# Columns of the second layer's h made before the LayerNorm, h in halves, and the small experts' outputs as split parts in a two-layer hybrid block

## The chip, the cores and the metric

The kernel runs on one core of a Trainium2 chip. The metric is the device time of one execution in microseconds (us), less is better. A core has five engines with their own instruction streams: TensorE (PE; its weight loads are shown as PEld), VectorE (DVE), ScalarE (ACT), GpSimd (POOL) and SyncE (SP), which here issues nearly all DMA transfers on one queue. They wait for one another by semaphores. TensorE's granted clock is given as a share of full speed.

## The reference

T = 256 tokens of width D = 1024, in float32, two layers. Each layer normalizes its tokens with an adaptive LayerNorm (scale and shift from `c @ w_ada + b_ada`), runs three mixers on the result (retention, a state-space mixer and sliding-window attention), projects their outputs back to D, adds the gated result to the input times ALPHA, and normalizes; then the same with a feed-forward part. Layer 0 has a dense SwiGLU of width 2816, layer 1 a mixture of 8 experts of width 3584, of which each token takes two:

```python
def _swiglu(h, wg, wu, wd):
    return (jax.nn.silu(h @ wg) * (h @ wu)) @ wd

def _moe(h, w_router, b_router, wg, wu, wd):
    ...
    top_v, top_i = lax.top_k(logits, TOP_K)
    top_w = jax.nn.softmax(top_v, -1)
    gates = jnp.sum(jax.nn.one_hot(top_i, N_EXPERTS, dtype=jnp.float32) * top_w[..., None], axis=1)
    out = jnp.zeros_like(t)
    for e in range(N_EXPERTS):
        out = out + gates[:, e:e + 1].astype(t.dtype) * _swiglu(t, wg[e], wu[e], wd[e])
    return out.reshape(Bn, L, D)
```

## The kernel before, in words

**Products.** An fp32 operand that is to be multiplied fast is split into two fp32r parts, the rounded value (a copy on ACT, L326) and what is left of it (a subtraction on DVE, L327). `mm3` (L395 to L397) then makes three matmuls: high by high, high by low, low by high. A matmul on fp32 operands as they are is one instruction that takes TensorE longer.

**Layer 0 and the boundaries.** Weights come in blocks of 1 MB over SP's queue into a ring of slots. `out_proj` and the end of `dense_ffn` call `follow(t, acc)` of `next_h` (L605) for each half t of the tokens. It forms the sum R, its statistics on DVE (L583 to L594), the reciprocal root on POOL (L575, L596) and the normalization on ACT (L603). For t = 1 it then makes the next h: `make_ht` calls `h_rows`, which transposes R in eight blocks on TensorE (L502), applies scale and shift from the columns `ac` (L508 on ACT, for k4 = 1 of t = 1 L510 on DVE), and after both halves `make_ht` writes the parts h1 (ACT, L491) and h2 (DVE, L492). `affine_cols` (L632) computes `ac` in a few tiny DVE instructions; at the second boundary (the end of the feed-forward part of layer 0) it is called from within `follow`. `affine_rows` (L626) then multiplies and shifts R itself on POOL (L623, L624), two instructions over 128x1024 for each t, with the rows in a tile of the tag "pair", which the gate rows (`ga`, L465) take next. These stretches run in the order in which they are written (a manual schedule), each engine by itself; the mixers are ordered by a scheduler. `behind()` adds an order of what is issued within it behind instructions named before; it works between instructions on one engine.

**The experts.** Tokens are gathered by rank of the experts. Four of them (ranks 1 to 4, called B) have up to 128 rows and weights that are split as above; the four others (ranks 0, 5, 6, 7, called S) have at most 64 rows and multiply by the raw fp32 weights, with two halves of the columns side by side on the partitions (`up_small` L1505, `down_small` L1537). Each expert has 7 steps of 6 blocks of 1 MB, 336 blocks in all. `plan` (L1318) writes the order of the steps: S S B B, then B and S in turn, at the end two steps of the last S alone. `feed` issues loads as slots come free. Side work is queued: `later(n, f)` runs f after n ticks, a tick follows each piece of a step, and a wide tick takes one job (a few matmuls into a bank C) from `jobs` and collects it at the next tick.

**An expert's output.** A B expert's y is scaled by the gates on POOL, split, and scattered to the tokens by one-hot matmuls (L1562). An S expert's y is scaled on DVE into `yts` (L1586) and scattered by four plain fp32 matmuls with 64 rows (L1591). Of the last B expert, `parts_of_last` (L1662) splits the sum so far and y, and `sums_of_last` (L1684) adds them in PSUM with 16 matmuls (L1692, L1696) right behind its last down step. The last S expert adds its four matmuls (L1776) to these banks, and `finish` normalizes and writes the output.

Of the kernel before, what the change touches and what calls it, by code (L numbers as in the profile page):

```python
# [42 lines left out]
SCALE_AT = 2  # L43

# [8 lines left out]
WIDE = {"": (2,), "S": (0, 1, 2, 3), "BS": (0, 1, 2, 3)}  # L53
# [113 lines left out]
def _layout(a):  # L167
# [16 lines left out]
    out["crow"] = a["c"]  # L184
    cm, ak, tm, zz = [], [], [], []
# [24 lines left out]
def block_stack_kernel(ctx: ExitStack, tc: tile.TileContext, I, out, coff, poff, cap=P):  # L210
# [42 lines left out]
    crep = W("crep").rearrange("p (k m) -> p k m", k=NK)  # L253
# [241 lines left out]
    def h_rows(hp, t, R, ac):  # L495

        hts = []
        for k4 in range(2):
# [12 lines left out]
            hts.append(ht)  # L511
        return hts
# [75 lines left out]
    def row_scale(st):  # L588
# [7 lines left out]
        nc.gpsimd.tensor_tensor(rs[:, 1:2], rs[:, 2:3], rs[:, 0:1], op=MULT)  # L596
# [551 lines left out]
    def route(hp, late, ahead, first, R, ac, g, xold):  # L1148
# [11 lines left out]
        def logits(t):  # L1160
            hts = h_rows(hp, t, R, ac)
# [156 lines left out]
    def plan(kind):  # L1318
# [6 lines left out]
        for c in ORDER[kind]:  # L1325
# [34 lines left out]
    def moe(mp, own, pair, hold, ahead, xs, sv, gate, cint, svr, gater, offi, room, big, ac, acc, gf):  # L1360
# [18 lines left out]
        def fetch(ex):  # L1379

            ex["rows"] = mp.tile([P, D], F32, tag="srows" if ex["small"] else "brows", name="rows", bufs=1)
            nc.gpsimd.indirect_dma_start(ex["rows"], None, xr, bass.IndirectOffsetOnAxis(ap=ex["ix"], axis=0))

        def turn_rows(ex, k4):

            ps = bankB()
            for c in range(4):
                k = 4 * k4 + c
                nc.tensor.transpose(ps[:, c * P:(c + 1) * P], ex["rows"][:, k * P:(k + 1) * P], ident)
# [27 lines left out]
        def slotted(ex, ps):  # L1417
# [5 lines left out]
            pt = mp.tile([P, 2, P], F32 if small else F32R, tag="pts" if small else "pt", name="pt", bufs=2)  # L1423
# [105 lines left out]
        def down_small(box, first, last, between=None, wide=False):  # L1529
            y = box["ex"]["y"]  # L1530
            for h in range(2):
# [8 lines left out]
                tick(wide)  # L1540

# [84 lines left out]
        def experts(kind):  # L1626
# [35 lines left out]
            def parts_of_last():  # L1662
# [13 lines left out]
                for j in range(2):  # L1676
                    s = slice(512 * j, 512 * j + 512)
                    yt = own.tile([P, 512], F32, tag=("yt", "yts")[j], name="yt")
# [20 lines left out]
            for op, r, b in ops[:-1]:  # L1699
# [34 lines left out]
                elif op == "Bturn":  # L1734
                    later(0, turned, box, turn(box))
                    while due:
                        tick()
# [11 lines left out]
                elif op == "Sup":  # L1749
                    boxes[r, b] = up_small(ex[r], WIDE.get(letter, ()))  # L1750
# [5 lines left out]
                elif op == "Sdown":  # L1756
# [6 lines left out]
                    if b == EX_STEPS - 1:  # L1763
                        later(0, output_small, ex[r])
# [7 lines left out]
            yt = own.tile([P, 512], F32, tag="yts", name="yt")  # L1772
            nc.vector.scalar_tensor_tensor(yt, small["y"], small["gs"], parts["gf2"], op0=MULT, op1=MULT)
            for t, j in itertools.product(range(2), range(2)):
                r = slice(64 * j, 64 * j + 64)
                nc.tensor.matmul(done[t, j], lhsT=small["pt"][r, t, :], rhs=yt[r, :], start=False, stop=True)  # L1776
# [69 lines left out]
    ada_pool = ada_scope.__enter__()  # L1846
    zb, quads = [], {}
# [73 lines left out]
    for l in range(2):  # L1921
# [27 lines left out]
        if l == 0:  # L1949
# [5 lines left out]
            def split_z():  # L1955
                ws.extend(split(I["wz"][1, 1, i], 4 * 324) for i in range(2))

            def ahead_z():
                box.append([bankA(), bankA()])
                tm_products(box[0], ws[0], 0, (0,), 324)  # L1960
# [13 lines left out]
            def zw():  # L1974
                for kh, t in ((1, 0), (0, 1), (1, 1)):
                    tm_products(box[0], ws[kh], kh, (t,), 324)
                return box[0]

            R = Rn2
            affine_rows(R, 0, 1)  # L1980
# [53 lines left out]
```

## Time and profile before

| | |
|---|---|
| median of 3 runs | 1399.26 us (1396.99 to 1399.78) |
| the profiled execution, its own time | 1399.08 us |
| its span, first to last instruction | 1397.2 us |
| mean granted clock of TensorE | 0.978 |
| PE / DVE / ACT / POOL busy | 96% / 66% / 47% / 6% |
| moved by DMA | 484.40 MB, mean 347 GB/s |

The profiled execution has 1.88 us outside its span. Layer 0 takes the first 396 us, the mixers and the routing of layer 1 the time up to about 510 us, the experts the rest. In all rows the first number is a start in us from the span's begin and the second a duration in us, if nothing else is said; "x8" joins eight instructions of one kind, and what stands in brackets is the idle time of the engine ahead of the row, and what ended it.

### The profile page before, as it was taken

To read this page: it belongs to the slowest core of one execution; us is meant where nothing else is said; L and a number is where in the kernel's file an instruction comes from. 1 tells how busy PE (TensorE), PEld (TensorE's weight loads), DVE (VectorE), ACT (ScalarE), POOL (GpSimd) and SP (SyncE) were. 2 spreads that over 40 slices of the span, in tenths; PEclk is the share of its full clock that TensorE was granted. 3 is DMA by queue.
4 is the path that set the end of the run, shared out by engine and by line. 5 is a ranking of instruction groups with operands and counts; after the bars stand their busy time and mean duration, and the time that the engine had idled before them with its cause. 6 is when DMAs were issued, how large, how long until landed. Compare 5 with 4: busy or idle time off the path is not lost. (4 is left out here: it accounts for less than half of the span.)

```text
span 1397.2 us, 20777 instructions
## 1 busy us (share of the span) xinstructions
PE 1335.7 (96%) x7956; PEld 1010.8 (72%) x7956; DVE 926.2 (66%) x1417; ACT 654.8 (47%) x948; POOL 88.7 (6%) x78
## 2 busy tenths in 40 slices
PE   7999899999899999999999999999999999999984
PEld 5867699999797885877676676677667777667641
DVE  3785789988778755956576665578556676665623
ACT  3743554453474533744454444456344555444510
POOL 0111020000121110003000000000000000000000
PEclk9999999999999978999999999999999999999998
DMA  9776668897543359999999999999999999999991
GB/s 388 291 297 244 250 241 330 353 382 284 202 168 127 109 223 392 383 368 410 417 420 421 420 421 420 421 421 420 421 421 420 420 421 421 421 420 421 421 397 43
DMA packets 69364, 484.40 MB, mean 347 GB/s; under 512 B 7744, under 2 KB 7744, under 8 KB 12800
## 3 DMA queue, kind: packets, MB, share of 16 engines
q1 hardware_dynamic: 67680, 477.41, 84.1%
q0 software_dynamic: 1568, 5.51, 1.1%
q8 instruction: 66, 1.08, 0.3%
q14 instruction: 50, 0.41, 0.1%
HBM read 480.52 MB, written 2.36 MB: 346 GB/s over the span
## 5 line engine op out<-in xcount | busy, mean ns | idle before, releaser
L327 DVE TENSOR_TENSOR w<-raw,w 128x1024 fp32r<-128x1024 f32 (+3 forms) x560 | 567.6, 1048 | 146.0 <-ACT w L326 137.9
L326 ACT ACTIVATE w<-raw 128x1024 fp32r<-128x1024 f32 (+3 forms) x560 | 484.7, 905 | 269.7 <-DMA raw<-in_wexp 110.9
L395 PE MATMUL B<-w,he 128*128 128x512 f32 x448 | 185.8, 415 | 3.2 <-ACT he L1404 3.2
L397 PE MATMUL B<-w,he 128*128 128x512 f32 x448 | 177.4, 396 | 0.0
L396 PE MATMUL B<-w,he 128*128 128x512 f32 x448 | 177.1, 395 | 0.0
L1505 PE MATMUL B<-raw,hs 128*64 128x256 f32 x1344 | 150.4, 382 | 0.0
L1505 PEld LDWEIGHTS B<-raw,hs 128*64 128x64 f32 x1344 | 95.1, 137 | 54.1 <-issue 6.3
L395 PE MATMUL A<-w,a 128*128 128x512 f32 x312 | 124.4, 399 | 0.0
L397 PE MATMUL A<-w,a 128*128 128x512 f32 x312 | 123.3, 395 | 0.0
L396 PE MATMUL A<-w,a 128*128 128x512 f32 x312 | 122.9, 394 | 0.0
L395 PEld LDWEIGHTS B<-w,he 128*128 128x128 f32 x448 | 84.7, 189 | 44.2 <-ACT w L326 18.7
L1518 DVE TENSOR_TENSOR sgs<-B,sgs 128x256 f32<-128x256 f32 x28 | 11.9, 425 | 150.8 <-ACT sgs L1515 150.8
L395 PE MATMUL B<-w,h 128*128 128x256 f32 (+1 forms) x368 | 107.1, 291 | 3.1 <-ACT h L491 3.1
L397 PE MATMUL B<-w,h 128*128 128x256 f32 (+1 forms) x368 | 106.0, 288 | 1.2 <-DVE h L492 1.1
L396 PE MATMUL B<-w,h 128*128 128x256 f32 (+1 forms) x368 | 105.5, 287 | 0.0
L1537 PE MATMUL A<-raw,as 128*64 128x512 f32 x448 | 101.5, 593 | 0.5 <-DVE as L1527 0.5
L1515 ACT ACTIVATE sgs<-B 128x256 f32<-128x256 f32 x28 | 10.7, 383 | 188.9 <-PE B L1505 188.9
L397 PEld LDWEIGHTS B<-w,he 128*128 128x128 f32 x448 | 84.6, 189 | 20.1 <-DVE he L1405 0.4
L396 PEld LDWEIGHTS B<-w,he 128*128 128x128 f32 x448 | 84.8, 189 | 15.8
L395 PE MATMUL A<-w,h 128*128 128x512 f32 (+1 forms) x176 | 68.6, 390 | 6.8 <-ACT h L491 4.4
L395 PEld LDWEIGHTS B<-w,h 128*128 128x128 f32 x368 | 71.5, 194 | 4.1 <-ACT h L491 3.3
L397 PEld LDWEIGHTS B<-w,h 128*128 128x128 f32 x368 | 71.4, 194 | 1.8 <-DVE h L492 1.8
(380 smaller groups left out, 1861.3 us busy)
## 6 DMA issues: line engine op xcount, KB each, us to landing
raw<-in_wexp SPq DMA_DIRECT2D x335, 1024.0 KB, 17.7
ada<-in_wada SPq DMA_DIRECT2D x45, 1024.0 KB, 6.6
raw<-in_wffn SPq DMA_DIRECT2D x33, 1024.0 KB, 7.2
raw<-in_wcm SPq DMA_DIRECT2D x8, 1024.0 KB, 6.9
raw<-in_wtm SPq DMA_DIRECT2D x8, 1024.0 KB, 6.8
raw<-in_wout SPq DMA_DIRECT2D x8, 1024.0 KB, 5.8
raw<-in_wz SPq DMA_DIRECT2D x8, 648.0 KB, 10.2
raw<-in_wada SPq DMA_DIRECT2D x3, 1024.0 KB, 11.6
```

Source lines behind the costliest of these rows:

```text
L326: nc.scalar.activation(w1[:, s], r, AF.Copy)
L327: eng.tensor_tensor(w2[:, s], r, w1[:, s].bitcast(F32), op=SUB)
L395: nc.tensor.matmul(ps, lhsT=a1, rhs=b1, start=start, stop=False, **kw)
L396: nc.tensor.matmul(ps, lhsT=a1, rhs=b2, start=False, stop=False, **kw)
L397: last["mm"] = nc.tensor.matmul(ps, lhsT=a2, rhs=b1, start=False, stop=stop, **kw)
L1505: nc.tensor.matmul(ps[64 * h:64 * h + 64, 256 * g:256 * g + 256], lhsT=ex["he"][k // 4][:, k % 4, :], rhs=raw[:, 512 * kk + 256 * h:512 * ...
L1515: nc.scalar.activation(box["sg"], ps[:, 0:256], AF.Silu)
L1518: nc.vector.tensor_tensor(box["sg"], ps[:, 256:512], box["sg"], op=MULT)
L1537: nc.tensor.matmul(y[64 * j:64 * j + 64, :], lhsT=box["a"][:, c, 64 * h:64 * h + 64], rhs=raw[:, 1024 * c + 512 * j:1024 * c + 512 * j + 512],
```

## The change

It has six parts. (1) The constant `crep` leaves the tile `par` and gets a tile and a load of its own. (2) `affine_cols(0, 1, 1, 0)` is called in `split_z`, ahead of the splits of the next weights, not within `follow`. (3) The two calls of `affine_rows` in layer 0 stand in `behind()`. (4) `h_rows` yields each half of h as soon as it is written, and `make_ht` splits it then. (5) For an expert with at most 64 rows, `fetch` takes 64 rows, not 128, and the transposes are 64 wide. (6) An S expert's y is scaled where it stands in PSUM, split into two fp32r parts that lie on the two halves of the partitions of one tile `st`, and scattered by one fp32r matmul of 128 rows for each of four outputs, with delays of `SMALL_AT` and `STEP_AT` ticks between the steps. At the end, the sums of the last B expert go behind the second-to-last `up` step of S, the `up` steps after the last B step take no jobs in their ticks (`WIDE["last"]`), and `down_small` collects a job right after the tick that issued it.

```diff
-    parts["crep"] = np.repeat(_cols(a["c"][0]), 32, axis=1)
...
+    out["crep"] = np.repeat(_cols(a["c"][0]), 32, axis=1)
...
-            hts.append(ht)
-        return hts
+            yield ht
...
-            nc.gpsimd.indirect_dma_start(ex["rows"], None, xr, bass.IndirectOffsetOnAxis(ap=ex["ix"], axis=0))
+            n = SMALL if ex["small"] else P
+            nc.gpsimd.indirect_dma_start(ex["rows"][0:n], None, xr, bass.IndirectOffsetOnAxis(ap=ex["ix"][0:n], axis=0))
...
             end = c == "S" and "Bturn" not in [op for op, _, _ in ops] and n["B"] == EX_STEPS * len(RANKS[kind]["B"])
             ops.append((c + "up", *at(c, i)))
+            if c == "S" and not end and "Bturn" in [op for op, _, _ in ops] and "sums" not in [op for op, _, _ in ops]:
+                ops.append(("sums", *at("B", n["B"] - 1)))
...
-            if end:
-                ops.append(("sums", *at("B", n["B"] - 1)))
...
                 tick(wide)
+                if wide:
+                    evacuate()
...
         def scaled_small(ex):
-            yt = own.tile([P, 512], F32, tag="yts", name="yts")
             for j in range(2):
                 r = slice(64 * j, 64 * j + 64)
-                nc.vector.scalar_tensor_tensor(yt[r, :], ex["y"][r, :], ex["gs"][r, :], gf[r, 512 * j:512 * j + 512], op0=MULT, op1=MULT)
-            ex["yt"] = yt
+                nc.vector.scalar_tensor_tensor(ex["y"][r, :], ex["y"][r, :], ex["gs"][r, :], gf[r, 512 * j:512 * j + 512], op0=MULT, op1=MULT)
+
+        def parts_small(ex, j):
+
+            r, o = slice(64 * j, 64 * j + 64), slice(64 - 64 * j, 128 - 64 * j)
+            st = ex["st", j] = own.tile([P, 512], F32R, tag=f"st{j}", name="st")
+            nc.scalar.copy(st[r, :], ex["y"][r, :])
+            nc.vector.tensor_tensor(st[o, :], ex["y"][r, :], st[r, :].bitcast(F32), op=SUB)
...
-            r = slice(64 * j, 64 * j + 64)
-            nc.tensor.matmul(ps, lhsT=ex["pt"][r, t, :], rhs=ex["yt"][r, :], start=True, stop=True)
-
-        def output_small(ex):
-            scaled_small(ex)
-            for j, t in itertools.product(range(2), range(2)):
-                jobs.append((lambda ps, j=j, t=t: scatter_small(ex, j, t, ps), lambda ps, j=j, t=t: collect(j, t, ps)))
+            nc.tensor.matmul(ps, lhsT=ex["pt"][:, t, :], rhs=ex["st", j], start=True, stop=True)
+
+        def output_small(ex, j=None):
+
+            if j is None:
+                scaled_small(ex)
+                return later(STEP_AT, output_small, ex, 0)
+            parts_small(ex, j)
+            later(STEP_AT, scatters_small, ex, j)
+
+        def scatters_small(ex, j):
+            for t in range(2):
+                jobs.append((lambda ps, t=t: scatter_small(ex, j, t, ps), lambda ps, t=t: collect(j, t, ps)))
+            if j == 0:
+                output_small(ex, 1)
...
-                    boxes[r, b] = up_small(ex[r], WIDE.get(letter, ()))
+                    boxes[r, b] = up_small(ex[r], WIDE["last"] if parts else WIDE.get(letter, ()))
...
-                        later(0, output_small, ex[r])
+                        later(SMALL_AT, output_small, ex[r])
...
             def split_z():
+                box.append(affine_cols(0, 1, 1, 0))
                 ws.extend(split(I["wz"][1, 1, i], 4 * 324) for i in range(2))
...
-            affine_rows(R, 0, 0)
+            with behind():
+                affine_rows(R, 0, 0)
...
-                next_h(wx[0], g_box["f"], R, Rn2, lambda: affine_cols(0, 1, 1, 0), ahead_z)(t, acc)
+                next_h(wx[0], g_box["f"], R, Rn2, lambda: box[0], ahead_z)(t, acc)
...
-            affine_rows(R, 0, 1)
+            with behind():
+                affine_rows(R, 0, 1)
```

How the order of the instructions changes, at three places. After the change most line numbers differ by one or two. First POOL at the second boundary of layer 0: L623 and L624 (before) are the affine rows of one half of the tokens, L575 and L596 the reciprocal root of the other half, CZ belongs to the next mixer. Before:

```order
L623 TENSOR_TENSOR R<-R,gb 128x1024
L624 TENSOR_TENSOR R<-R,gb 128x1024
L575 TENSOR_TENSOR rs<-rs,cst 128x1
L596 TENSOR_TENSOR rs<-rs 128x1
L623 TENSOR_TENSOR R<-R,gb 128x1024
L624 TENSOR_TENSOR R<-R,gb 128x1024
L710 MEMSET CZ 128x512
```

The same place after the change:

```order
L622 TENSOR_TENSOR R<-R,gb 128x1024
L623 TENSOR_TENSOR R<-R,gb 128x1024
L574 TENSOR_TENSOR rs<-rs,cst 128x1
L595 TENSOR_TENSOR rs<-rs 128x1
L622 TENSOR_TENSOR R<-R,gb 128x1024
L623 TENSOR_TENSOR R<-R,gb 128x1024
L709 MEMSET CZ 128x512
```

Nothing moved here: the affine rows of t = 0 still stand ahead of the root for t = 1.

Next ACT at the same boundary, R being the normalization, h and h_88 the fp32 h and its high part, gf and ga gate rows. Before:

```order
L603 ACTIVATE R<-R,rs 128x512 x2
L465 ACTIVATE gf<-C 128x512 x2
L508 ACTIVATE h_3815<-B,ac 128x128 x4
L508 ACTIVATE h_3825<-B,ac 128x128 x4
L491 CAST h_88<-h_3815 128x4x128
L491 CAST h_88<-h_3825 128x4x128
L603 ACTIVATE R<-R,rs 128x512 x2
L508 ACTIVATE h_3855<-B,ac 128x128 x4
L491 CAST h_88<-h_3855 128x4x128
L491 CAST h_88<-h_3865 128x4x128
```

After:

```order
L602 ACTIVATE R<-R,rs 128x512 x2
L508 ACTIVATE h_3817<-B,ac 128x128 x4
L466 ACTIVATE gf<-C 128x512
L492 CAST h_88<-h_3817 128x4x128
L508 ACTIVATE h_3829<-B,ac 128x128 x4
L466 ACTIVATE gf<-C 128x512
L492 CAST h_88<-h_3829 128x4x128
L602 ACTIVATE R<-R,rs 128x512 x2
L508 ACTIVATE h_3857<-B,ac 128x128 x4
L492 CAST h_88<-h_3857 128x4x128
L466 ACTIVATE ga<-C 128x512
L492 CAST h_88<-h_3869 128x4x128
```

Each cast now follows its own four activations, a gate row stands between the activations and the cast of each half, and `ga`, which was later before, stands ahead of the last cast.

Last PE at the end of the experts: L1505 is an `up` half step of the last S expert, L1537 a `down` step, L1523 the transposes of its activations, and w with `one` and `pt` the 16 matmuls of `sums_of_last`. Before:

```order
L1537 MATMUL A<-raw,as 64x512 x8
L1692 MATMUL A<-w,one 128x512 x2
L1692 MATMUL B<-w,one 128x512 x2
L1692 MATMUL A<-w,one 128x512 x4
L1696 MATMUL A<-w,pt 128x512 x2
L1696 MATMUL B<-w,pt 128x512 x2
L1696 MATMUL A<-w,pt 128x512 x4
L1505 MATMUL B<-raw,hs 64x256 x32
L1523 MATMUL C<-cst,sgs 128x128 x2
L1537 MATMUL A<-raw,as 64x512 x8
L1505 MATMUL B<-raw,hs 64x256 x32
```

After (the sums are L1707 and L1711):

```order
L1537 MATMUL A<-raw,as 64x512 x8
L1505 MATMUL B<-raw,hs 64x256 x32
L1707 MATMUL A<-w,one 128x512 x2
L1707 MATMUL B<-w,one 128x512 x2
L1707 MATMUL A<-w,one 128x512 x4
L1711 MATMUL A<-w,pt 128x512 x2
L1711 MATMUL B<-w,pt 128x512 x2
L1711 MATMUL A<-w,pt 128x512 x4
L1537 MATMUL A<-raw,as 64x512 x4
L1523 MATMUL C<-cst,sgs 128x128 x2
L1537 MATMUL A<-raw,as 64x512 x4
```

The sums moved behind an `up` step, and the transposes stand between two halves of a `down` step.

## Rows read from the trace of the kernel before

**Rows 1.** The profile's page: its first line, the busy time of each engine, and, of the span in 40 slices of 34.9 us, what the DMA engines moved in each.

```profile
span 1397.2 us, 20777 instructions
PE 1335.7 (96%) x7956; PEld 1010.8 (72%) x7956; DVE 926.2 (66%) x1417; ACT 654.8 (47%) x948; POOL 88.7 (6%) x78
...
GB/s 388 291 297 244 250 241 330 353 382 284 202 168 127 109 223 392 383 368 410 417 420 421 420 421 420 421 421 420 421 421 420 420 421 421 421 420 421 421 397 43
```

**Rows 2.** Stretches of the span: from and to, length, then busy time (and count) of PE, PEld, DVE, ACT and POOL, the granted clock, the DMA share and GB/s.

```profile
173.00:180.00 7.00, 6.12 (x28) 5.89 (x29) 1.29 (x2) 2.76 (x5) 5.24 (x4) 0.52 0.31 106
...
381.00:388.00 7.00, 5.41 (x21) 5.14 (x22) 1.29 (x2) 4.19 (x10) 0.00 (x0) 0.51 0.01 2
580.00:610.00 30.00, 30.00 (x167) 21.22 (x166) 17.76 (x18) 15.47 (x18) 0.00 (x0) 1.00 0.83 318
700.00:1338.00 638.00, 634.00 (x3476) 441.82 (x3478) 404.95 (x461) 308.01 (x346) 13.45 (x10) 1.00 1.01 421
...
1350.00:1354.00 4.00, 4.00 (x38) 2.51 (x36) 0.00 (x0) 0.00 (x0) 0.00 (x0) 0.95 0.82 320
```

**Rows 3.** What the queue of SP waited for between 700 and 1350 us: the line and the tile whose use had to end, us in total, times, longest.

```profile
SPq L303 <- DMA raw<-in_wexp: 265.0, 155, 3.2
SPq L303 <- PE B L1505: 142.6, 69, 8.6
```

**Rows 4.** The timeline's first issue of SP and the first matmuls.

```profile
0.75 0.40 SPq L236 DMA_DIRECT2D par<-in_par  x1
...
7.29 1.94 PE L425 MATMUL B<-ada,par 128*32 128x256 f32 x16 [7.29 <-DMA ada<-in_wada]
```

**Rows 5.** The timelines at the first boundary (end of the mixers of layer 0): two rows of ACT, two of PE, one of DVE.

```profile
170.43 2.90 ACT L508 ACTIVATE h<-B,ac 128x128 f32<-128x128 f32 x8 [0.96 <-PE B L502]
173.18 1.17 ACT L491 CAST h<-h 128x512 fp32r<-128x512 f32 x2
...
173.88 0.58 PE L395 MATMUL B<-w,h 128*128 128x256 f32 x1 [3.06 <-ACT h L491]
...
182.40 4.11 DVE L492 TENSOR_TENSOR h<-h,h 128x512 fp32r<-128x512 f32 x2 [0.38 <-ACT h L491]
```

**Rows 6.** The timelines at the second boundary (end of the feed-forward part of layer 0): three rows of DVE, one of ACT, three of POOL, two of PE.

```profile
375.55 1.09 DVE L636 TENSOR_TENSOR ac<-par,modc 128x8 f32<-128x8 f32 x1
376.56 0.15 DVE L637 TENSOR_TENSOR ac<-par,modc 128x8 f32<-128x8 f32 x1
...
376.79 2.39 DVE L638 TENSOR_TENSOR ac<-ac,modc 128x8 f32<-128x8 f32 x2
...
389.47 4.48 DVE L492 TENSOR_TENSOR h<-h,h 128x512 fp32r<-128x512 f32 x2
...
376.41 0.60 ACT L465 ACTIVATE gf<-C 128x512 f32<-128x512 f32 x1 [1.25 <-PE C L461]
379.14 2.90 ACT L508 ACTIVATE h<-B,ac 128x128 f32<-128x128 f32 x8 [2.13 <-DVE ac L638]
...
374.22 2.40 POOL L623 TENSOR_TENSOR R<-R,gb 128x1024 f32<-128x1024 f32 x1 [2.40 <-ACT R L603]
376.69 2.38 POOL L624 TENSOR_TENSOR R<-R,gb 128x1024 f32<-128x1024 f32 x1
...
388.20 2.39 POOL L623 TENSOR_TENSOR R<-R,gb 128x1024 f32<-128x1024 f32 x1 [8.34 <-PE B L502]
...
382.59 0.64 PE L395 MATMUL A<-w,h 128*128 128x324 f32 x1 [4.38 <-ACT h L491]
...
394.00 0.42 PE L397 MATMUL A<-w,h 128*128 128x324 f32 x1 [0.75 <-DVE h L492]
```

**Rows 7.** PE's timeline around two scatter matmuls of an S expert (L1591), among a `down` step of a B expert.

```profile
1001.51 0.40 PE L396 MATMUL A<-w,a 128*128 128x512 f32 x1
1001.75 0.40 PE L397 MATMUL A<-w,a 128*128 128x512 f32 x1
1002.08 1.12 PE L1591 MATMUL C<-yts,pt 64*128 64x512 f32 x2
...
1003.47 0.39 PE L396 MATMUL A<-w,a 128*128 128x512 f32 x1
```

**Rows 8.** PE's timeline at the end of the experts, and two rows of DVE from there.

```profile
1338.62 0.49 PE L1692 MATMUL A<-w,one 128*128 128x512 f32 x1
...
1348.83 7.90 PE L1505 MATMUL B<-raw,hs 128*64 128x256 f32 x64
1357.68 0.44 PE L1523 MATMUL C<-cst,sgs 128*128 128x128 f32 x2 [0.95 <-DVE sgs L1518]
...
1361.53 7.08 PE L1505 MATMUL B<-raw,hs 128*64 128x256 f32 x64
...
1373.09 3.65 PE L1537 MATMUL A<-raw,as 128*64 128x512 f32 x16 [0.53 <-DVE as L1527]
...
1341.35 0.75 DVE L1679 SCALAR_TENSOR_TENSOR yt<-A,gslot,gf 128x512 f32<-128x512 f32 x1
1342.85 0.69 DVE L1681 TENSOR_TENSOR w<-yt,w 128x512 fp32r<-128x512 f32 x1 [0.76 <-ACT w L1680]
```

**Rows 9.** The last load of a weight block: its issue (duration in ns, start in us) and the us from issue to landing.

```profile
L303 SPq DMA_DIRECT2D raw<-in_wexp x1: 333/333/333, 1353.3 to 1353.3; - x1
...
DMA to landing us min/median/max: 8.7/8.7/8.7
```

More of the change, by code (lines that the diff above doesn't have):

```diff
@@ L43 @@
 SCALE_AT = 2
+SMALL_AT = 5
+STEP_AT = 3
 FIRST_BLOCKS = (0, 1, 2, 3, 6, 7, 8, 9, 4, 5)
@@ L52 @@
 SMALL = 64
-WIDE = {"": (2,), "S": (0, 1, 2, 3), "BS": (0, 1, 2, 3)}
+WIDE = {"": (2,), "S": (0, 1, 2, 3), "BS": (0, 1, 2, 3), "last": ()}
 PAIR_AT = (2, 4, 9, 25)
@@ L252, in block_stack_kernel @@
     ident, mle, mgt = C("ident"), C("mle"), C("mgt")
-    crep = W("crep").rearrange("p (k m) -> p k m", k=NK)
     def slab(tag, name):
@@ L595, in row_scale @@
         rsqrt(rs[:, 0:1], rs[:, 1:2])
-        nc.gpsimd.tensor_tensor(rs[:, 1:2], rs[:, 2:3], rs[:, 0:1], op=MULT)
+        last["rs"] = nc.gpsimd.tensor_tensor(rs[:, 1:2], rs[:, 2:3], rs[:, 0:1], op=MULT)
         return rs
@@ L1160, in logits @@
         def logits(t):
-            hts = h_rows(hp, t, R, ac)
+            hts = list(h_rows(hp, t, R, ac))
             for k in range(NK):
@@ L1381, in fetch @@
             ex["rows"] = mp.tile([P, D], F32, tag="srows" if ex["small"] else "brows", name="rows", bufs=1)
-            nc.gpsimd.indirect_dma_start(ex["rows"], None, xr, bass.IndirectOffsetOnAxis(ap=ex["ix"], axis=0))
+            n = SMALL if ex["small"] else P
+            nc.gpsimd.indirect_dma_start(ex["rows"][0:n], None, xr, bass.IndirectOffsetOnAxis(ap=ex["ix"][0:n], axis=0))
         def turn_rows(ex, k4):
-            ps = bankB()
+            ps, n = bankB(), SMALL if ex["small"] else P
             for c in range(4):
                 k = 4 * k4 + c
-                nc.tensor.transpose(ps[:, c * P:(c + 1) * P], ex["rows"][:, k * P:(k + 1) * P], ident)
+                nc.tensor.transpose(ps[:, c * P:c * P + n], ex["rows"][0:n, k * P:(k + 1) * P], ident[0:n, 0:n])
             later(0, turned_rows, ex, k4, ps)
@@ L1422, in slotted @@
                 fetch(ex)
-            pt = mp.tile([P, 2, P], F32 if small else F32R, tag="pts" if small else "pt", name="pt", bufs=2)
+            pt = mp.tile([P, 2, P], F32R, tag="pts" if small else "pt", name="pt", bufs=2)
             nc.vector.tensor_copy(pt.rearrange("p t n -> p (t n)"), ps[:, 0:256])
@@ L1677, in parts_of_last @@
                     s = slice(512 * j, 512 * j + 512)
-                    yt = own.tile([P, 512], F32, tag=("yt", "yts")[j], name="yt")
+                    yt = own.tile([P, 512], F32, tag=("yt", "st0")[j], name="yt")
                     nc.vector.scalar_tensor_tensor(yt, e["y"][j], e["gs"], gf[:, s], op0=MULT, op1=MULT)
@@ L1736, in experts @@
                     while due:
-                        tick()
+                        tick(False)
                 elif op == "Bdown":
@@ L1771, in experts @@
             down_small(boxes[S[-1], EX_STEPS - 1], False, True)
-            yt = own.tile([P, 512], F32, tag="yts", name="yt")
+            yt = own.tile([P, 512], F32, tag="st1", name="yt")
             nc.vector.scalar_tensor_tensor(yt, small["y"], small["gs"], parts["gf2"], op0=MULT, op1=MULT)
@@ L1775, in experts @@
                 r = slice(64 * j, 64 * j + 64)
-                nc.tensor.matmul(done[t, j], lhsT=small["pt"][r, t, :], rhs=yt[r, :], start=False, stop=True)
+                nc.tensor.matmul(done[t, j], lhsT=small["pt"][r, t, :].bitcast(F32), rhs=yt[r, :], start=False, stop=True)
             finish(lambda t, j: done[t, j])
@@ L1846, in block_stack_kernel @@
     ada_pool = ada_scope.__enter__()
+    crep = ada_pool.tile([P, NK, 32], F32, name="crep", bufs=1)
+    nc.sync.dma_start(out=crep.rearrange("p k m -> p (k m)"), in_=I["crep"])
     zb, quads = [], {}
@@ L1959, in ahead_z @@
                 box.append([bankA(), bankA()])
[L1960 removed]
+                tm_products(box[1], ws[0], 0, (0,), 324)
             pre, ws, box = [], [], []
@@ L1975, in zw @@
                 for kh, t in ((1, 0), (0, 1), (1, 1)):
-                    tm_products(box[0], ws[kh], kh, (t,), 324)
-                return box[0]
+                    tm_products(box[1], ws[kh], kh, (t,), 324)
+                return box[1]
             R = Rn2
-            affine_rows(R, 0, 1)
+            with behind():
+                affine_rows(R, 0, 1)
             less_w(*wx)
```

1 line of the change is left out of this document (removed).

## The prediction

> **What bounds the kernel now.** I read the page first: TensorE is busy for 96% of the span, and from the eighteenth slice on DMA moves 410 to 421 GB/s with hardly a change [rows 1]. Two resources look full, so the stretches must say which of them sets the end where. In the middle of the experts (700 to 1338 us) both are: PE busy 634 of 638 us at full clock, DMA share 1.01 at 421 GB/s [rows 2]. The waits of SP show that the queue is not starved by itself: most of its waiting is for a transfer to land, but 142.6 us go to slots that an `up` product of S had not yet freed [rows 3]. Early in the experts (580 to 610 us) it is PE alone: busy throughout, DMA at 318 GB/s [rows 2]. So there, and in layer 0, a PE wait that goes shifts all that follows. The last block is issued at 1353.3 and lands 8.7 later, at 1362.0 [rows 9], while the last `down` step ends at 1373.09 + 3.65 = 1376.74 [rows 8]: the products run behind the stream by 14.7 us at the end, and only a part of that is needed for the last step. My reading is that the stream carries this part and that PE adds its lateness at the end.
>
> **The change part by part,** against the profiled execution's 1399.08 us (span 1397.2, 1.88 around it; it lies 0.2 us under the median of 1399.26).
>
> *crep.* The queue gets one issue more ahead of the first weights. An issue took 0.40 us, and the first matmuls start when the first of these lands, at 7.29 [rows 4]. Bytes are the same. I take +0.4 (0 to 0.5).
>
> *First boundary.* PE waits 3.06 us until 173.88 for the casts, and on ACT both stand behind all eight activations of 2.90 us, so a first cast now comes 4 x 0.36 = 1.4 us sooner [rows 5]. But the products of the second half of the tokens end late for another reason: the two DVE subtractions took 4.11 us from 182.40 [rows 5], where two of that shape take 1.3 unhindered, and POOL's rows, which lie there, keep their place. So of the 1.4 I count 1.0 gained (0 to 2). In this stretch the granted clock was 0.52, the lower level of 1.2 GHz, after PE's wait [rows 2]. If the shorter wait keeps it at the upper one, up to 3 us more go; I leave that to the range.
>
> *Second boundary.* Here the columns came late. L636 took 1.09 us against 0.15 of its neighbour L637, and L638 2.39 for two; the latter ended with POOL's second affine row, at 376.69 + 2.38 = 379.07, and only then did ACT begin h, at 379.14 [rows 6]. PE sat idle 4.38 us until 382.59. With the columns made before, ACT can begin when the transposes are there, about 374.8, and the first cast ends near 374.8 + 1.45 + 0.6 + 0.6 (a gate row between them) = 377.4: the first product is 5.2 us sooner. The third matmul of each triple needs the DVE subtraction too, which meets POOL's L624. If it comes first it takes 0.65 us, otherwise it ends at 379.07 + 0.65 = 379.7. So PE is 2.8 to 5.2 us ahead here, and the transposes of t = 1, which released POOL at 388.20 [rows 6], end at about 383.8.
> Then a new wait comes in. The order shows POOL unchanged: the behind() has no effect on an engine whose named predecessors are on ACT and DVE. So POOL runs the affine rows of t = 1 directly behind the transposes, 2.39 + 2.73 = 5.1 us (the second by its kind's row at the first half, 2.38, would be 4.8). And `ga`, now ahead of the last cast on ACT, needs the tile that these rows hold. Behind it queue the last cast, and behind that the last subtraction and PE's last products: 383.8 + 5.1 + 0.6 (ga) + 0.6 (cast) + 0.7 (subtraction) = 390.8, where before this subtraction released PE at 394.00 [rows 6]. That is 3.2 us; the issue between the steps costs some, so I take −3.0 (−1.5 to −5).
> The Trainium skill's page "SBUF — State Buffer", section Who interferes with whom, says that a DVE instruction with two SBUF inputs contends with a GpSimd instruction that reads SBUF, and that whoever issues first holds the shared ports for the whole instruction. The trace agrees (1.09 and 2.39 us against 0.15, ending with POOL's rows). The rule speaks against this part of the change, as POOL's rows keep their places: by it, with POOL first, the term is the low end of the range, −1.5.
>
> These three sum to +0.4 − 1.0 − 3.0 = −3.6. The shift reaches the experts whole, as PE has no slack in front of them.
>
> *Fetch.* Three S experts (ranks 5, 6, 7) fetch 64 rows instead of 128: 3 x 64 x 4 KB = 0.79 MB less, at 421 GB/s −1.9 us of the stream.
>
> *Outputs of S.* A plain fp32 matmul is recorded as two passes, and the scatter of 64 rows at 1002.08 is such a pair: from the last start ahead of it, 1001.75, to 1003.47 PE took 1.72 us for it and two ordinary steps, which follow one another after 0.24 [rows 7]. So one scatter costs 1.24 us. One fp32r matmul costs 0.24, −1.0 for each of the 3 x 4 (three S experts, four outputs): −12.0 us of PE. On the other engines ACT gets two casts and DVE two subtractions per expert, all of some 0.7 us; ACT and DVE are busy 308 and 405 of 638 us there [rows 2] and hide them. The narrower transposes I count at nothing (0 to −2.6).
>
> *End.* The 16 sums take 1338.62 to 1348.83, 10.2 us, because they wait for the splits. At 0.24 each they take 3.8 behind an `up` step, with their operands ready: −6.4. The `up` step took 7.90 against 7.08 for its like that follows [rows 8]: −0.8. The wait ahead of the transposes at 1357.68, 0.95, goes under half a `down` step: −1.0. Together −8.2. The gap in the loads at 1350 to 1354 (320 of 421 GB/s in 4 us, [rows 2]) goes too, since the slots behind the sums come free sooner: −1.0 of the stream.
>
> *Which of these counts.* PE sheds 12.0 + 8.2 = 20.2 us, but cannot end its last product before the last block is there. That is at 1362.0, and half a `down` step, 1.9, and some 2 us (0 to 3) of turning are left: 1365.9, or 10.8 us less than 1376.74. With the stream's own −1.9 and −1.0 the experts give −13.7. PE's 20.2 exceed that by 6.5, which is the cushion under new waits in this part. If PE is never let past the stream, the remaining 6.5 us are lost to waits for blocks.
>
> Sum: −3.6 − 13.7 = −17.3, so 1399.08 − 17.3 = 1381.8.
>
> **The rivals.**
> A is the forecast, with a range of its own of 1378 to 1386 (from the bounds of the two boundaries and of the last step).
> B: the 421 GB/s is no ceiling but what the freed slots allow, since 142.6 us of SP's waiting are for slots that PE holds [rows 3]. Then PE's savings count whole: 1399.08 − 3.6 − 20.2 = 1375.3. Against it stands that 421 does not move through twenty slices [rows 1]. The Trainium skill's "DMA: Bandwidth & Descriptors", section Where 436 GB/s comes from, puts the ceiling of the ports at 435 GB/s; by that the stream could go 3% faster at most, which by itself would speak for A.
> C: the outputs of S give nothing, their twelve us being eaten by waits of the longer chain (scale, cast, subtract, each some ticks apart): 1399.08 − 3.6 − 8.2 = 1387.3.
> D: the boundaries give nothing, as `ga` waits for POOL as long as was gained: 1399.08 + 0.4 − 13.7 = 1385.8.
> E: no change that can be told, 1399: the end only changes what PE waits for, and the scatters were hidden.
> F, slower: y of an S expert is now scaled in place, so its bank (one, shared by all S experts) is held until both parts are made: 2 x 0.75 (scale) + 2 x 0.6 (cast) + 2 x 0.69 (subtract) [rows 5, 8] = 4.1 us plus 5 + 3 + 3 ticks. The first `down` step of the next S expert must wait for it, with all of PE's order behind. It decides from 9 us at each of the three places: 27 less the cushion of 6.5, against 17.3 gained, +3.2, or 1402.3. For it: a tick is a piece of a step, and a few us long. Against it: between the last `down` of one S expert and the first of the next lie two S and one B step, some 16 ticks.
>
> **How the numbers follow.** A .52, B .12, C .13, D .07, E .07, F .09. About 0.2% (2.8 us) is what a measurement of this kernel can tell from no change. A to D are faster by more: .84; E same: .07; F slower: .09. The range runs from under B, with the boundaries' clock, 1373, to 1393, past C and D with a new wait of 5 us; E and F stay outside.
>
> **What would show it.** Right: at the first boundary the first cast follows four activations; at the second PE's idle time falls from 4.38 us to under 2, the last release there names ACT's ga behind POOL and comes near 391; scatters 0.24 apart; the sums in one run of about 4 us; DMA at 421 GB/s to a last landing near 1355.5 (1362.0 − 3.6 − 2.9); last `down` end near 1359.4, 4 us behind it. Wrong: DMA above 425 (B); PE waits on DVE or ACT at y's bank before a first `down` of S (F) or between scatters (C); the last product still 10 us behind the landing.

## The result, and the profile after

The changed kernel takes 1391.92 us (median of 5 runs, 1390.37 to 1392.45) against 1398.89 of the kernel before in the same session: ratio 0.9949, 95% interval [0.9937, 0.9961]. It is 7.0 us faster where 17.3 had been forecast. The profiled execution took 1391.49 us, its span is 1389.7.

The first lines of its page, as in [rows 1]:

```profile
span 1389.7 us, 20769 instructions
PE 1324.4 (95%) x7944; PEld 1008.5 (73%) x7944; DVE 922.9 (66%) x1423; ACT 656.8 (47%) x954; POOL 89.2 (6%) x78
...
GB/s 380 283 294 270 227 242 335 335 367 323 223 173 124 127 207 365 388 356 421 393 420 421 420 421 419 410 420 421 420 421 420 421 408 421 420 421 421 420 421 121
```

PE lost 11.3 us of work (1335.7 to 1324.4), close to the 12.0 of the scatters. The stream still runs at 421 GB/s, but its twentieth, twenty-sixth and thirty-third slices have 393, 410 and 408, where the kernel before has 417, 421 and 421 [rows 1]. The three fetches of 64 rows fall into these slices. What SP's queue waited for between 700 and 1350 us, as in [rows 3]:

```profile
SPq L304 <- DMA raw<-in_wexp: 446.0, 232, 3.6
SPq L304 <- PE B L1505: 32.4, 22, 6.8
```

The waits for slots held by PE fell from 142.6 to 32.4 us and those for landings rose from 265.0 to 446.0, and the rate did not rise: the freed slots were no limit, so rival B is out. PE had come nearer to the stream. The end of the experts, with the rows of [rows 8] and what stands around them: PE of the changed kernel, then the ACT rows that PE waits for:

```profile
1322.89 0.66 PE L1477 MATMUL B<-cst,sg 128*128 128x128 f32 x4
1326.23 0.80 PE L396 MATMUL A<-w,a 128*128 128x512 f32 x1 [2.68 <-ACT a L1483]
...
1335.75 3.65 PE L1537 MATMUL A<-raw,as 128*64 128x512 f32 x16
...
1346.24 0.73 PE L1707 MATMUL A<-w,one 128*128 128x512 f32 x2
...
1349.13 1.10 PE L1711 MATMUL A<-w,pt 128*128 128x512 f32 x4
...
1365.72 3.65 PE L1537 MATMUL A<-raw,as 128*64 128x512 f32 x16 [0.53 <-DVE as L1527]
...
1320.93 2.00 ACT L327 ACTIVATE w<-raw 128x1024 fp32r<-128x1024 f32 x2 [10.04 <-DMA raw<-in_wexp]
1323.43 2.00 ACT L327 ACTIVATE w<-raw 128x1024 fp32r<-128x1024 f32 x2 [0.49 <-DMA raw<-in_wexp]
...
1325.60 0.57 ACT L1483 CAST a<-B 128x512 fp32r<-128x512 f32 x1
```

Six us of it as a stretch, columns as in [rows 2]:

```profile
1327.00:1333.00 6.00, 5.59 (x15) 4.07 (x14) 0.81 (x2) 2.51 (x5) 0.00 (x0) 0.50 1.01 421
```

The same place in the kernel before:

```profile
1327.65 0.66 PE L1477 MATMUL B<-cst,sg 128*128 128x128 f32 x4
...
1335.04 3.65 PE L1537 MATMUL A<-raw,as 128*64 128x512 f32 x16
...
1319.42 2.01 ACT L326 ACTIVATE w<-raw 128x1024 fp32r<-128x1024 f32 x2 [4.67 <-DMA raw<-in_wexp]
```

This is the last step of the last B expert. L1477 turns its activations, and the S `down` step of 16 passes (L1537) follows its 24 products. Before, PE came to the turn at 1327.65 and to L1537 7.4 us later. Now PE comes at 1322.89, 4.8 us sooner, but the cast of the turned activations stands on ACT behind the splits of both weight blocks, and the second of these waits for its landing. PE waits 2.7 us, its clock then falls to 0.50, the lower level of 1.2 GHz, until 1333, and L1537 comes 12.9 us after the turn: at 1335.75, 0.7 us later than before. The whole lead of 4.8 us, and this 0.7, is gone at this one place. From L1537 on the end runs 33.6 us to its last product at 1369.37, against 41.7 before: that is −8.1.

The second loss lies ahead of the experts. Windows of the changed kernel at the end of layer 1's mixers, and the ACT rows there:

```profile
476.00:482.00 6.00, 2.92 (x11) 2.00 (x12) 4.86 (x12) 4.46 (x15) 1.01 (x1) 0.81 0.52 175
482.00:488.00 6.00, 6.00 (x25) 4.88 (x24) 4.17 (x7) 1.12 (x2) 0.00 (x0) 0.91 0.41 142
```

```profile
475.61 0.41 ACT L1008 ACTIVATE junk<-ys 128x256 f32<-128x256 f32 x1
...
477.21 1.05 ACT L1032 CAST h<-B 128x512 fp32r<-128x512 f32 x2
...
477.82 0.50 PE L396 MATMUL A<-w,h 128*128 128x512 f32 x1 [1.97 <-ACT h L1032]
```

The same two places in the kernel before:

```profile
478.78 0.58 ACT L1033 CAST h<-B 128x512 fp32r<-128x512 f32 x1
479.27 0.42 ACT L1009 ACTIVATE junk<-ys 128x256 f32<-128x256 f32 x1
...
479.42 0.50 PE L395 MATMUL A<-w,h 128*128 128x512 f32 x1 [0.24 <-ACT h L1033]
```

L1032 casts the transposed outputs of the mixers, for which PE now waits 2.0 us. It stands behind the four sums of squares (L1008); in the kernel before, its first cast stood ahead of them, 0.7 us after its transposes' start, and PE waited 0.24 us. Another wait of 0.78 us follows at 479.33 in the changed kernel, and the granted clock falls: 0.81 is the mean of six us, and from 480 to 482 it is 0.50, the lower level. Between the transposes of the mixed tokens and those of the next LayerNorm pass 29.2 us (474.76 to 503.96), before 26.0 (478.09 to 504.07).

### The profile page after: what moved, and what is told of

Same layout as the page of the kernel before. It is cut to its first block, busy times and chain, and to the rows that moved or that the text cites. A ratio compares the mean times of both kernels' runs of the same rounds, so it can differ in the third digit from the quotient of the medians.

```text
span 1389.7 us, 20769 instructions
## 1 busy us (share of the span) xinstructions
PE 1324.4 (95%) x7944; PEld 1008.5 (73%) x7944; DVE 922.9 (66%) x1423; ACT 656.8 (47%) x954; POOL 89.2 (6%) x78
## 5 line engine op out<-in xcount | busy, mean ns | idle before, releaser
L327 ACT ACTIVATE w<-raw 128x1024 fp32r<-128x1024 f32 (+3 forms) x560 | 484.5, 905 | 343.4 <-DMA raw<-in_wexp 158.0
L1505 PE MATMUL B<-raw,hs 128*64 128x256 f32 x1344 | 149.6, 380 | 0.0
L1505 PEld LDWEIGHTS B<-raw,hs 128*64 128x64 f32 x1344 | 94.9, 137 | 53.5 <-issue 7.4
L1537 PE MATMUL A<-raw,as 128*64 128x512 f32 x448 | 101.7, 593 | 0.5 <-DVE as L1527 0.5
L396 PEld LDWEIGHTS B<-w,h 128*128 128x128 f32 x368 | 71.2, 193 | 4.1 <-ACT h L492 2.7
L398 PEld LDWEIGHTS B<-w,h 128*128 128x128 f32 x368 | 71.1, 193 | 2.0 <-DVE h L493 1.9
L397 PEld LDWEIGHTS B<-w,h 128*128 128x128 f32 x368 | 71.2, 194 | 0.4
L396 PEld LDWEIGHTS A<-w,a 128*128 128x128 f32 x312 | 59.3, 190 | 15.7 <-ACT a L1483 2.9
## 6 DMA issues: line engine op xcount, KB each, us to landing
raw<-in_wada SPq DMA_DIRECT2D x3, 1024.0 KB, 12.9
```

Of the source, the lines that this page charges most:

```text
L327: nc.scalar.activation(w1[:, s], r, AF.Copy)
L396: nc.tensor.matmul(ps, lhsT=a1, rhs=b1, start=start, stop=False, **kw)
L397: nc.tensor.matmul(ps, lhsT=a1, rhs=b2, start=False, stop=False, **kw)
L398: last["mm"] = nc.tensor.matmul(ps, lhsT=a2, rhs=b1, start=False, stop=stop, **kw)
L1505: nc.tensor.matmul(ps[64 * h:64 * h + 64, 256 * g:256 * g + 256], lhsT=ex["he"][k // 4][:, k % 4, :], rhs=raw[:, 512 * kk + 256 * h:512 * ...
L1537: nc.tensor.matmul(y[64 * j:64 * j + 64, :], lhsT=box["a"][:, c, 64 * h:64 * h + 64], rhs=raw[:, 1024 * c + 512 * j:1024 * c + 512 * j + 512],
```

## The experiments

Two numbers of each run's trace carry the argument: when ACT begins to split the first block of the last B step (L327), which it does on landing in every run, and when the last S product ends; "rest" is the difference of the two. The last column is the median of the run's executions, the others are starts and ends in its one profiled execution.

| run | first S product | split | last product ends | rest | time |
|---|---|---|---|---|---|
| before | 524.6 | 1319.4 | 1376.7 | 57.3 | 1398.9 |
| changed | 524.1 | 1320.9 | 1369.4 | 48.4 | 1391.9 |
| e1 plain outputs | 527.5 | 1324.7 | 1374.8 | 50.1 | 1394.8 |
| e2 end only, on before | 523.4 | 1318.2 | 1367.5 | 49.4 | 1390.2 |
| e3 fetch of 128 rows | 524.4 | 1320.8 | 1368.4 | 47.6 | 1391.0 |
| e4 casts ahead | 518.7 | 1315.5 | 1364.2 | 48.6 | 1387.5 |
| e5 plain outputs, crep back in par | 523.6 | 1321.1 | 1371.1 | 50.0 | 1392.6 |
| e6 cast in the tail | 524.0 | 1321.4 | 1365.0 | 43.6 | 1387.3 |
| e7 four mended | 517.0 | 1312.5 | 1356.1 | 43.6 | 1379.1 |
| e8 crep on ACT's queue | 522.4 | 1319.3 | 1366.7 | 47.4 | 1391.0 |
| e9 less bytes | 524.4 | 1316.6 | 1364.3 | 47.7 | 1386.5 |
| e10 rows behind root | 523.6 | 1320.5 | 1369.1 | 48.6 | 1392.9 |
| e11 boundaries, on before | 524.5 | 1320.3 | 1376.0 | 55.7 | 1397.4 |
| e12 all but outputs | 517.5 | 1313.1 | 1364.4 | 51.4 | 1386.6 |

From the first S product to the split pass 794.8 to 797.5 us in every run but e9. The first S product moves from one profiled execution to the next by up to 3.4 us (e1, e3 and the changed kernel are one program up to there), so differences of a run's time under 2 us are read from the trace, not from the median. The median of the kernel before lay between 1398.2 and 1398.9 us whenever a group of runs was measured beside it.

**Plain outputs (e1).** All of the S outputs' edits undone.

```diff
-            nc.tensor.matmul(ps, lhsT=ex["pt"][:, t, :], rhs=ex["st", j], start=True, stop=True)
+            nc.tensor.matmul(ps, lhsT=ex["pt"][r, t, :], rhs=ex["yt"][r, :], start=True, stop=True)
```

> The changed kernel, but the S experts' outputs as before (plain fp32 scatters of 64 rows); all else stays. Theory S (the end is set by the landing of the last B block and by PE's work behind it; PE's savings ahead of that only turn into waits): about the changed kernel's time, 1391.9 us (1390 to 1394), PE waits less behind the last S up step ahead of the last B down step. Rival P (PE's savings count wherever they are made): 12 us come back, 1404.

It measured 1394.8 us, ratio to before 0.9964 [0.9951, 0.9978]. That is 0.8 us above the range of theory S and 9 us under P. Its profiled execution began the experts 3.4 us later, where the two programs are one; the rest is 1.7 us longer, not 12: P falls.

**The end alone (e2).** The kernel before with the plan of the sums, the ticks and the collect of the end.

```diff
-                ops.append(("sums", *at("B", n["B"] - 1)))
...
+            if c == "S" and not end and "Bturn" in [op for op, _, _ in ops] and "sums" not in [op for op, _, _ in ops]:
+                ops.append(("sums", *at("B", n["B"] - 1)))
```

> The kernel before with the end's edits alone (sums behind the second-to-last up step, no jobs in the ticks after the last B step, the collect right behind its tick). Theory S: the whole gain of the end, 8.2 us by the prediction's rows, so 1390.7 (1389 to 1392), as fast as the whole change or faster. Rival P: the end is only one part of the gain of 7.0, so 1394 to 1397.

It measured 1390.22 us, ratio 0.9946 [0.9933, 0.9958]. The part on the end alone makes the whole gain; the rest of the change adds nothing that these times can tell.

**Fetch of 128 rows (e3).**

```diff
-            nc.gpsimd.indirect_dma_start(ex["rows"][0:n], None, xr, bass.IndirectOffsetOnAxis(ap=ex["ix"][0:n], axis=0))
+            nc.gpsimd.indirect_dma_start(ex["rows"], None, xr, bass.IndirectOffsetOnAxis(ap=ex["ix"], axis=0))
```

> The changed kernel, but every fetch takes 128 rows again. Theory F (a fetch of 64 rows holds the weight stream up as long as one of 128, and the stream loses rate beside it: 248 to 373 GB/s in the stretches of 2 us there, against 421): the last weight blocks land about 1 us sooner, 1390.8. Rival (bytes count, as the prediction had it): 1.9 us later, 1393.8.

It measured 1390.98 us, ratio 0.9943 [0.993, 0.9956]; 0.9 us is within the noise. The traces tell it apart. The stretch of one fetch of 64 rows in the changed kernel, and of the same fetch of 128 rows in the kernel before (the last column is GB/s):

```profile
886.20:890.40 4.20, 4.20 (x20) 3.38 (x19) 3.44 (x4) 1.50 (x2) 0.00 (x0) 1.00 1.02 321
```

```profile
891.00:895.80 4.80, 4.80 (x22) 3.89 (x21) 3.29 (x4) 1.35 (x2) 0.00 (x0) 1.00 1.01 415
```

Half the rows take nearly as long, and in that time all traffic falls to 321 GB/s with the DMA engines busy throughout. The lost rate costs 4.2 x 100 / 421 = 1.0 us, more than the 0.6 us of the bytes saved. Over the whole stream, from the first S product to the landing of the last block, pass 839.1 us in the mean of the seven profiled kernels with 64 rows (838.3 to 839.9, e9 left out) and 837.8 in that of the six with 128 (837.4 to 838.6). These kernels differ in other parts too, so the 1.3 us between them is only near the price of the three fetches.

**Crep (e5, e8).** In e5 the load is undone, which for want of memory goes only with plain outputs; in e8 it stays, on another queue.

```diff
-    nc.sync.dma_start(out=crep.rearrange("p k m -> p (k m)"), in_=I["crep"])
+    nc.scalar.dma_start(out=crep.rearrange("p k m -> p (k m)"), in_=I["crep"])
```

> As the run with plain outputs, and crep back in the tile par, so one issue less ahead of the first weights. Theory: the load of its own costs 1.4 us at the start (the products of layer 0 start 1.43 later in the changed kernel's trace), all of it carried to the end: 1.4 us less than the run with plain outputs. Rival (the prediction's 0.4): 0.4 us less.

> The changed kernel with the load of crep issued by ACT and not by SP. Theory: the first products of layer 0 start 1.5 us sooner (they stood at 27.0 to 28.3 us with crep's load on SP and at 25.0 to 26.2 without it), carried to the end: 1390.4. Rival (the bytes matter, not the issue): no change, 1391.9.

They measured 1392.62 (0.9954 [0.9941, 0.9967]) and 1391.02 us (0.9951 [0.9936, 0.9966]), neither told apart from its counterpart by time. The first matmul of the changed kernel and of e8, as in [rows 4]:

```profile
8.62 1.93 PE L426 MATMUL B<-ada,crep 128*32 128x256 f32 x16 [8.62 <-DMA ada<-in_wada]
```

```profile
7.32 1.94 PE L426 MATMUL B<-ada,crep 128*32 128x256 f32 x16 [7.32 <-DMA ada<-in_wada]
```

So 1.3 us go where one issue of 0.4 had been counted: the first weights, for which this matmul waits, land later. The start itself varies: it lies at 8.1 to 9.1 in the seven profiled kernels with crep's load on SP's queue and at 6.9 to 7.7 in the seven others.

**Casts ahead in layer 1 (e4).** The sums of squares written behind the first casts.

```diff
             small_mix(yw, 6)
+            if l == 1:
+                norm_z()
             small_mix(yr, 0)
```

> The changed kernel with the sums of squares of layer 1's state-space mixer written behind the first casts of the mixed tokens, so that ACT makes that cast first, as in the kernel before. Theory M (of the 3.3 us that the two boundaries won, 3.2 to 4.5 are lost between the transposes of the mixed tokens and the next LayerNorm, because PE waits 2.1 us for casts behind eight activations and its clock then falls to 0.81): that stretch is 26 us long again instead of 29 to 30.5, the first product of the experts starts 3 us sooner and the end comes 3 us sooner, 1389. Rival (the stretch is lost for another reason, the landing of weights): 1391.9.

It measured 1387.54 us, ratio 0.9921 [0.9908, 0.9935]: 4.4 us under the changed kernel. Its windows against those above:

```profile
476.00:482.00 6.00, 6.00 (x30) 4.64 (x29) 5.47 (x13) 3.57 (x7) 1.01 (x1) 1.00 0.56 179
482.00:488.00 6.00, 6.00 (x27) 4.87 (x26) 1.48 (x3) 0.00 (x0) 0.00 (x0) 1.00 0.75 274
```

PE is busy throughout at full clock, the stretch takes 25.4 us (472.77 to 498.2) instead of 29.2, and the shift reaches the end. This settles the second loss: it was the order of ACT. Not all of the gain is this order's, though: the last product ends 5.2 us sooner than in the changed kernel, and 2.0 us of lead were there ahead of the stretch, 1.3 of them because at the first boundary the granted clock stayed at 1.00 from 176 to 180, where the changed kernel has 0.59.

**Boundaries alone (e11).** The kernel before with `affine_cols` early and h by halves.

```diff
+                box.append(affine_cols(0, 1, 1, 0))
...
+            yield ht
```

> The kernel before with the boundaries' edits alone (columns made early, h by halves). Theory M: 3.3 to 4 us sooner at the start of layer 1's mixers, lost again between the transposes of the mixed tokens and the next LayerNorm (30 us instead of 26), so 1398.5 (1397 to 1400). Rival (the shift reaches the end, as the prediction had it): 1394.9.

It measured 1397.44 us, ratio 0.9991 [0.9982, 1.0]: rival D's picture of this part, though not by D's wait. Its order has the casts behind the sums of squares as well, and the stretch takes 30.5 us. So the boundaries' own edits bring on the loss: with them the tile scheduler, which orders the mixers, places other work first. Why it does so was not looked into.

**Rows behind the root (e10).**

```diff
-            with behind():
+            with behind(last["rs"]):
                 affine_rows(R, 0, 1)
```

> The changed kernel, but POOL's affine rows in layer 0 really queued behind the reciprocal root of the second half of the tokens (the behind() names that root). Theory Q (at the second boundary the normalization of the second half waits for POOL's rows of the first half, until 381.98 us in the changed kernel's trace, and the last cast waits for the rows of the second): the normalization begins 3 us sooner, the last cast 2 us sooner, layer 1 starts 2 us sooner and the end comes 2 us sooner, 1390. Rival (the rows only move into the way of the last cast): no change, 1391.9.

It measured 1392.9 us, ratio 0.9957 [0.9942, 0.9971], not told apart from the changed kernel. The normalization of the second half did begin 2.9 us sooner (379.08 against 382.02), but the last cast moved only from 390.08 to 388.37, as ga waits for both halves' rows. Of these 1.7 us 0.9 were left at the next LayerNorm, behind mixers with the same late casts (30.0 us for the stretch of 29.2), 0.5 at the first S product and 0.2 at the last.

**Cast in the tail (e6).** The last B step's second block is split behind the cast of its activations.

```diff
-                elif self.n["w"] < n and near:
+                elif self.n["w"] < min(n, self.most) and near:
...
+                feed.most = 2 if ops[at_op + 1][0] == "Bturn" else W_HALVES
```

> The changed kernel, but the splits of the last B step's second block come behind the cast and subtraction of its activations on ACT and DVE. Theory S (what follows the landing of the last B block sets the end): PE's wait of 2.7 us there goes and with it the half clock behind it, the down step of S behind it starts 5 us sooner (49.5 us from landing to end become 45 to 46), 1387.5. Rival (PE would only meet the stream's last block): 1391.9; the last block lands at 1365.0 in the changed kernel's trace, 4.4 us ahead of the last product's end, so at most 2 to 3 us could go, 1389.5.

It measured 1387.33 us, ratio 0.9914 [0.9899, 0.993]: 4.6 us under the changed kernel. PE and ACT there:

```profile
1323.39 0.66 PE L1478 MATMUL B<-cst,sg 128*128 128x128 f32 x4
1324.72 0.50 PE L397 MATMUL A<-w,a 128*128 128x512 f32 x1 [0.67 <-ACT a L1484]
...
1331.42 3.65 PE L1538 MATMUL A<-raw,as 128*64 128x512 f32 x16
...
1321.42 2.00 ACT L327 ACTIVATE w<-raw 128x1024 fp32r<-128x1024 f32 x2 [10.03 <-DMA raw<-in_wexp]
...
1324.08 0.58 ACT L1484 CAST a<-B 128x512 fp32r<-128x512 f32 x1 [0.20 <-PE B L1478]
```

The wait falls from 2.68 to 0.67 us, the granted clock stays at 1.00 (1325 to 1333), and from the turn to the S step pass 8.0 us instead of 12.9. The rest falls to 43.6, by the same 4.8. The expectation's rival allowed too little: the last block lands at 1363.1 in the changed kernel, not at 1365.0, so the time alone does not rule it out. The trace does, as behind the turn PE waits for no block in either kernel. In e6 the last product ends 1.4 us behind the last landing (1363.6), so that landing, the forecast's bound, is now close.

**Less bytes (e9).** Four blocks in the middle loaded by half.

```diff
+                        if 120 <= self.count < 124:
+                            nc.sync.dma_start(out=raw[:, 0:1024], in_=src()[:, 0:1024])
```

> The changed kernel with four weight blocks in the middle of the experts loaded by half (2.1 MB less; that half of these weights isn't loaded and what stood in the slot is used). Theory S: the last B block lands 5.0 us sooner and the end comes 5.0 us sooner, 1386.9. Rival P (PE bounds this stretch): no change, 1391.9.

It measured 1386.54 us, ratio 0.9915 [0.9901, 0.9928]: 5.4 us less for 5.0 us of stream. In the changed kernel the stream bounds the middle of the experts.

**Four mended (e7) and all but the outputs (e12).** e7 joins e3, e4, e6 and e8. e12 does so with plain outputs, crep in par and the rows behind the root.

> The changed kernel with four things mended together: crep's load issued by ACT, fetches of 128 rows, layer 1's casts ahead of the sums of squares, and the casts of the last B step ahead of its second split. Theory S and M with the parts as measured one by one (crep 1 to 2, fetch 1.2, casts 3 to 4.4, tail 4.4): they add up, as all of them move either the landing of the last B block or what is behind it, so 1391.9 - 11 = 1381 (1379 to 1384). Rival (they overlap, the last block's landing becomes the bound): 1385.

> As the run with four things mended, but with plain outputs of S, so crep stays in par, and with POOL's rows behind the root. Theory S (the S experts' fp32r parts save PE time that the stream hides): as fast as the run with four mended things or up to 2 us faster, 1379 to 1381. Rival P: 12 us slower, 1392.

e7 measured 1379.12 us, ratio 0.9861 [0.9846, 0.9877]: faster than both kernels, 12.8 us under the changed one. Its clock at the first boundary stayed at 1.00 as in e4, and its last product too ends within 1.5 us of the last landing. e12 measured 1386.61, ratio 0.9917 [0.9903, 0.9931], where theory S had 1379 to 1381. The last B step in e7, then in e12:

```profile
1314.53 0.66 PE L1482 MATMUL B<-cst,sg 128*128 128x128 f32 x4
...
1322.47 3.65 PE L1542 MATMUL A<-raw,as 128*64 128x512 f32 x16
...
1312.50 2.00 ACT L327 ACTIVATE w<-raw 128x1024 fp32r<-128x1024 f32 x2 [10.03 <-DMA raw<-in_wexp]
```

```profile
1323.20 0.66 PE L1483 MATMUL B<-cst,sg 128*128 128x128 f32 x4
...
1330.79 3.65 PE L1543 MATMUL A<-raw,as 128*64 128x512 f32 x16
...
1313.05 2.01 ACT L328 ACTIVATE w<-raw 128x1024 fp32r<-128x1024 f32 x2 [2.74 <-DMA raw<-in_wexp]
```

With plain outputs PE reaches the turn 10.2 us after the first split, with parts 2.0 us. So theory S was too strong. The S outputs' saving does count, 7.5 us here (0.5 of it is there at the first S product, from the two other differences), once PE no longer throws its lead away at the turn; in the changed kernel it counted 1.7.

## Why the prediction was wrong, point by point

- *crep*, +0.4: mis-sized. The first matmul came 1.33 us later, the products of layer 0 1.43.
- *First boundary*, −1.0: right. The products were 2.22 us late ahead of it and 1.25 behind it, so −0.97, and seven other profiled kernels with these edits have −0.96 to −0.98, e11 −0.89. PE's wait fell from 3.06 to 1.81 us, and the DVE subtractions of the second half again met POOL's rows (2.53 us for one at 182.65). The clock, left to the range, decides more: in e4 and e7, where it stayed at 1.00, the step is −2.2, and in e1, where it was 0.57 from 176 to 184, it is +0.5. The net from crep's 1.43 to 1.25 is only −0.2, because 0.8 us had been lost just ahead, at the end of layer 0's mixers (granted clock 0.66 from 150 to 153, before 1.00). Two other profiled executions lost as much there, the rest 0.3 or less, so this differs from execution to execution.
- *Second boundary*, −3.0: right in mechanism and size. The shift went from +1.1 to −2.5 us, so −3.7. The waits came as said:

```profile
377.35 0.40 PE L396 MATMUL A<-w,h 128*128 128x324 f32 x1
...
389.59 0.60 ACT L466 ACTIVATE ga<-C 128x512 f32<-128x512 f32 x1 [3.85 <-POOL R L623]
390.08 0.61 ACT L492 CAST h<-h 128x512 fp32r<-128x512 f32 x1
...
390.72 0.69 DVE L493 TENSOR_TENSOR h<-h,h 128x512 fp32r<-128x512 f32 x1 [2.13 <-ACT h L492]
...
379.55 1.75 DVE L493 TENSOR_TENSOR h<-h,h 128x512 fp32r<-128x512 f32 x1 [1.05 <-ACT h L492]
```

  The first product was 5.2 us sooner, ga waited for POOL, and the last subtraction came at 390.7. The rule of the Trainium skill's "SBUF — State Buffer" (Who interferes with whom) held again (1.75 us beside POOL's rows, shown above, against 0.69 alone), but a whole row of 2.4 us was not waited for here, so the low end of the range did not come.
- *"The shift reaches the experts whole, as PE has no slack in front of them"*: failed. Of 3.3 us won by the transposes of layer 1's mixed tokens 3.2 were lost by the next LayerNorm. PE had no slack, but the order of ACT changed in the mixers, which a scheduler sets, and I had read the order at the boundaries only (e4, e11).
- *Fetch*, −1.9: wrong sign. Rate was lost beside the fetch, and the stream is some 1.3 us longer with 64 rows (e3).
- *Outputs of S*, −12.0 of PE: the saving is there (PE busy −11.3), but it did not reach the end. *End*, −8.2: measured −8.1.
- *"PE cannot end its last product before the last block is there ... 1365.9"*: failed, and it is the step that kept the outputs' saving from counting. I took the last block for the place where PE meets the stream. PE meets it first at the last B block, 16 blocks earlier, behind whose splits the cast of its operands stands; behind that landing lie 41 us (e6) to 46 us (here, 1323.3 to 1369.4) of PE work that no earlier saving shortens. There PE's lead of 4.8 us turned into a wait of 2.7 us and half clock. So the last product ended 6.3 us behind the last landing, where 3.9 had been added up; without the wait (e6) it is 1.4. The last block was indeed issued 7.5 us sooner and did not land sooner, as the queue ahead of it was full:

```profile
L304 SPq DMA_DIRECT2D raw<-in_wexp x3: 332/333/333, 1341.2 to 1345.8; - x3
...
DMA to landing us min/median/max: 17.3/18.5/19.4
```

  1345.8 + 17.3 is 1363.1, against 1362.0 before: the −1.0 for the gap in the loads did not come either.

Of the −17.3, then: the experts gave −6.8 (845.3 us from the first S product to the last, against 852.1) instead of −13.7, and what lies ahead of them −0.55 instead of −3.6. The 6.9 us missing in the experts are 4.5 of the stream (first S product to last landing: 837.4 us before, 839.0 now, 834.5 by the forecast's −2.9) and 2.4 behind the last landing. Three steps failed, then: the shift (3.1 us short, mostly by the order of ACT in layer 1's mixers), the stream's term (4.5 us short, most of it by the sign of the fetch) and the place where PE meets the stream (2.4 us short). A slip without weight: the rate of 410 to 421 GB/s holds from the nineteenth slice on, as the eighteenth has 368 [rows 1]. Rival C had the right time of the outputs (nearly nothing) and not the reason: not the chain of scale, cast and subtract held PE up, the turn of the last B step did. F's price at y's bank shows in no wait of PE.

## What to carry to other kernels

Where a stream and an engine are both full, look for the last block that the engine must have at once, not only for the last block: in this kernel what lies behind its landing was the only stretch in which saved engine work counted from the first. A lead is worth nothing if the first thing that it meets is a cast queued behind a split of data that has not landed; mend the order there first, then save work (1.7 us for the outputs before that, 7.5 after). And where a scheduler places a later stage, read its order there too, since an edit far ahead can move a cast behind work that nobody waits for.

## What the runs showed of the hardware

A gather of 64 rows of 4 KB occupied the DMA engines nearly as long as one of 128 rows (4.2 against 4.8 us), and all traffic fell from 415 to 321 GB/s beside it; which resource it holds is not shown. At the end of the experts a PE wait of 2.68 us was followed by six us at a granted clock of 0.50 (1.2 GHz); in the kernel e6, with a wait of 0.67 us at the same place, the clock stayed at 1.00. The longer wait cost 5.5 us in all (12.9 against 7.4 in the kernel before), twice its length. In layer 1's mixers waits of 1.97 and 0.78 us, up to 479.3, came ahead of a fall to 0.50 (480 to 482).
